# Two column groups of the recurrence moved from narrow blocks with stationary activations into one early wide block that TensorE turns

## The chip, the cores and the metric

The kernel runs on one core of a Trainium2 chip. The metric is the device time of one execution in microseconds (us); of the kernel before there are three runs, with a median of 1683.52. Engines are called as in the profile: PE (TensorE matmul), PEld (its weight load), DVE (VectorE), ACT (ScalarE), POOL (GpSimd) and SP (the queue that issues most DMAs).

## The reference

One decoder layer in float32 over 256 positions of width 2048. Cut to what matters:

```python
a = rmsnorm(h, norm_mix_pre)
proj = a @ w_in                       # 2048 x 17408
q_a, k_a, v_a, q_r, f_r, i_r, g_r, gate_a, gate_r = split_columns(proj)
attn = dilated_window_attention(...)  # three groups of 8 heads, rotary q and k
q_h = silu(q_r);  f = lb + (1 - lb) * sigmoid(f_r)
r_out = hgrn2_chunked(q_h, log(f), 1 - f, i_r)     # 8 heads of 128
r_out = rmsnorm(r_out) * gain * silu(g_r)
y = sigmoid(gate_a) * (attn @ w_attn_branch) + sigmoid(gate_r) * (r_out @ w_hgrn_branch)
h = h + rmsnorm(y @ w_mix_out)
g, u = split(rmsnorm(h) @ w_ffn_gate_up)
h = h + rmsnorm((silu(g) * u) @ w_ffn_down)
```

The row scale of the first norm is applied to the products, not to the operand. The change is about q_r and f_r, 1024 columns each, of which the kernel handles "half 0" (heads 0 to 3, 512 columns of each) and "half 1" apart.

## The kernel before, in words

All products are made in three matmuls of a high and a low part (x·w high, x·w low, low x·w high), so weights are split as they come in: ACT copies the high part out of the raw tile and DVE subtracts to get the low one (L355 and L356 for blocks of 256 columns, L390 and L410 for wide ones). The work is a list of blocks, each a list of steps over the contraction dimension; a step's matmuls are issued by `multiply` or `multiply_wide`, and behind each step the program advances the evacuations of finished blocks (`evacs`), two "lanes" of vector work (`lanes`, in which recurrence and attention run as generators, a piece a step), and, for steps in the range `ready_in`, one list of DMAs on POOL ("ready sums").

- A **wide block** (`Wide`) makes 1024 columns for all 256 positions in 8 steps. The activations are the stationary operand, so the result has positions on the partitions. A step "8" is 24 matmuls of 512 columns; a step "7" forms seven products of sums of quarters instead of eight (21 matmuls), which needs sums of weight quarters: SP loads the raw tile, POOL adds another quarter onto it with an accumulating DMA (L303), DVE adds (`sum`, L404 and L405), ACT and DVE split it into `dh` and `dl` (L415, L418). At the end of a block `gather` (L522 to L531) combines the seven products into a tile `e`, and `add_up` (L540) adds the others. Two sets of PSUM banks, `acc` and `aux`, change roles from block to block (`flip`). The early wide blocks make gate_a, gate_r, v and i; `evac_kept` (L812, L813) applies the function on ACT and writes `e` to DRAM by POOL ("kept"). From there it is read back (`back`, L803) when it is needed.
- A **W block** makes 256 columns in 4 steps of 512 rows with the weights stationary and the activations moving, so that the result has channels on the partitions and time along the row, as the recurrence and attention want it. A step is 16 matmuls. The blocks W#1 to W#4 are f and q_r of half 0 (`evac_f`, `evac_qr`), W#5 to W#8 those of half 1; 24 more make rotary q and k. At W#1 `end_early` closes the early stage's memory and opens the middle stage's, whose tiles take its place. At the end of W#4 `recurrence(0)` enters lane 0; its first DVE instruction makes kk = 1 − f (L1002).
- Then come the two branch products, the mix (`w_mix_out`, two wide blocks with POOL's raw additions) and the feed-forward stage (two narrow and ten wide blocks, then two wide ones of the down projection). In the feed-forward stage PE turns activations by transposes (L1454). Some of its seven steps use sums that were made in DRAM beforehand, the ready sums: three copies and three accumulating DMAs each, 256 KB a DMA (L446, L450), made in the 83 units from W#1 on that `ready_in` names. Their order against other POOL work is fixed by the place where the program issues them.

Of the kernel before, what the change touches and what calls it, by code (L numbers as in the profile page):

```python
# [39 lines left out]
def order(steps):  # L40

    k = steps.count("7")
    return [(steps[:i].count(x) + k * (x == "8"), int(x == "7")) for i, x in enumerate(steps)]


EARLY = [order(x) for x in ["88878878"] + ["87878787"] * 6 + ["88787878"]]
FFN = [order(x) for x in ["88878787"] + ["87877877", "87877877", "87877877", "87877877", "87877877", "87877877", "87877877", "87877877", "87877877"]]
DOWN = [[((n + 16 * j) % 22, n in by7) for n in range(KF // 2)] for j, by7 in enumerate( ([4, 6, 8, 10, 12, 14, 16, 18], [0, 2, 4, 6, 8, 10, 12, 14, 16, 18]))]

# [4 lines left out]


N_F = 16
KEPT_P, KEPT, KEPT_H = (18,), (6, 10), (16,)
READY, PACE, FIRST_READY, LAST_READY = {(2, 1), (2, 3), (3, 1), (3, 3), (4, 1), (4, 3), (5, 1), (5, 3), (6, 1), (6, 3), (7, 1), (7, 3), (8, 1), (8, 3), (9, 1), (9, 3), (10, 1), (10, 3), (11, 6), (11, 10), (11, 14), (12, 4), (12, 8), (12, 12), (12, 16)}, (4, 6), 2, 85


class Block:
# [48 lines left out]
def tile_hybrid_block(ctx: ExitStack, tc: tile.TileContext, t, out):  # L110
# [145 lines left out]
    def add_seven(*args, flip, whole=True, stage=None, **kw):  # L256
        b = Wide(*args, **kw)
        b.flip, b.whole, b.unit0, b.stage = flip, whole, len(units), stage
        b.plus = stage == "ffn"
        blocks.append(b)  # L260
        for i in range(b.steps):
            seq.append(Step(b, i, len(units), 0))
            units.append([seq[-1]])
# [309 lines left out]
    class Split:  # L573


        def __init__(self, s, nk, slot=rslot):
            self.flat = [slot(s) for _ in range(nk // 2)]
            self.slots = [x.rearrange("p (k z t) -> p k z t", k=2, z=2) for x in self.flat]
            self.there = set()

        def __call__(self, k):
            x = self.slots[k // 2]
# [222 lines left out]
    def evac_kept(key, fn):  # L805
        def go(b):
            dst = keep(key, 1024)
            add_up(b)
            yield
            for s in range(2):  # L810
                e = b.rest[:, 2 * s : 2 * s + 2].rearrange("p g c -> p (g c)")
                nc.scalar.activation(e, e, fn, scale=r1c[:, s : s + 1])  # L812
                nc.gpsimd.dma_start(dst[:, s, :], e)  # L813
                yield
        return go

    def end_early():
        flush(evacs)
        enter("middle")
        attnT.append(Split("attnT", 8))  # L820
        recT.append(Split("recT", 8))
        for half in range(2):
            gN[half] = hslot("g")
            back(gN[half], ("g", half), 0, 512, True)
            iN[half] = hslot("v")
            back(iN[half], "i", 512 * half, 512 * half + 512, True)
        for key, shape in (("lmask", [P, len(LEVELS), 64]), ("amask", [P, 2, 512])):
            masks[key] = pool["now"].tile(shape, F32, name=key)
            nc.gpsimd.dma_start(masks[key], t[key])

    def values_back(half):

# [11 lines left out]
    def evac_f(half):  # L844
        def ev(i, src):
            while "lb" not in ready:
                yield
            if i == 0:
                fT[half] = fslot("f").rearrange("p (h t) -> p h t", h=4)
            dst = fT[half]  # L850
            d = dst[:, 2 * i : 2 * i + 2, :]
            nc.vector.tensor_mul(in_time(d), by_side(src), by_side(by_rows(rowb, 2)))
            yield
            nc.scalar.activation(d, d, AF.Sigmoid)
            yield
            for h in (2 * i, 2 * i + 1):
                g = 4 * half + h
                nc.vector.tensor_scalar(
                    dst[:, h, :], dst[:, h, :], lb1[:, g : g + 1], lb[:, g : g + 1],
                    op0=OP.mult, op1=OP.add,  # L860
                )
        return ev

    def evac_qr(half, then=None):
        def ev(i, src):
# [119 lines left out]
    def recurrence(half):  # L985
# [175 lines left out]
        for j in range(2):  # L1161
            ps = aux()
            for h in range(2):
                for i in range(2):
                    hs = slice((2 * j + h) * P, (2 * j + h + 1) * P)
                    nc.tensor.transpose(
                        ps[:, h * S + i * P : h * S + (i + 1) * P], rt[:, i, hs], ident
                    )
            recT[0].put(2 * half + j, ps.rearrange("p (h t) -> p h t", h=2), True)
            if j == 1:  # L1170
                values_back(half)
            yield
# [258 lines left out]
    def aslot(s):  # L1431

        n = len(act_t)
        if len(H7) > 4 and n in (8, 9):
            x = hslot(s).rearrange("p b c -> p (b c)")
        else:
            x = rslot(s).bitcast(F32) if n < 8 else p3(s, F32, 1024, 1 if len(H7) > 4 else 3)
        return x.rearrange("p (k t) -> p k t", k=4)

    def turn_act(u, b):  # L1440

        dst = aslot("act")
        act_t.append(dst)
        side = "aux" if b.flip else "acc"
        pair = pair_of(side) if b.whole else [bank_of(side) for _ in range(2)]
        return lambda: turn_into(dst, pair, u, b.whole)
# [167 lines left out]
    for half in range(2):  # L1614
# [2 lines left out]
            post=more_x if half == 0 else None)  # L1617
    early = [(COL_GA, ("a", 0), AF.Sigmoid), (COL_GB, ("r", 0), AF.Sigmoid),
             (COL_GA + 1024, ("a", 1), AF.Sigmoid), (COL_GB + 1024, ("r", 1), AF.Sigmoid)]
    early += [(COL_V + 1024 * g, ("v", g), AF.Copy) for g in range(3)] + [(COL_IR, "i", AF.Copy)]  # L1620
    for n, (col, key, fn) in enumerate(early):
        add_seven(w_in, (col, col + 512), EARLY[n], xT, lambda m: x7[m],
                  evac_kept(key, fn), flip=n % 2 == 1, whole=n < 7, turn=1 if n else 6,
                  pre=({0: lambda: advance(evacs), 1: lambda: flush(lanes[1])}).get(n))
    for half in range(2):
        add_wide(w_in, KD, COL_FR + 512 * half, xT, evac_f(half))
        if half == 0:
            blocks[-2].pre = end_early
        add_wide(w_in, KD, COL_QR + 512 * half, xT, evac_qr(half, start_recurrence(half)))
    for pair in range(4):  # L1630
        for g in range(3):
            for o, col, tab in ((0, COL_Q, 0), (2, COL_K, 2)):
                then = start_attention(pair) if o and g == 2 else None
                add("W", w_in, KD, col + 1024 * g + 256 * pair, xT,
                    both_halves(evac_rope((pair, g), o, tab, then), 0))
    blocks[-3].pre = lambda: (gate_back("r", 0), gate_back("r", 1))
    for j in range(4):
        add("N", t["w_hgrn_branch"][0], 8, 512 * j, lambda k: recT[0](k), evac_rec_branch(j))
# [28 lines left out]
        st.n = n  # L1667
    for j, b in enumerate(blocks[mix_last + 3 :], 1):
        b.plus = any(k == j for k, _ in READY)
    ready_in = range(blocks[10].unit0 + FIRST_READY, blocks[10].unit0 + LAST_READY)  # L1670
    before = sums_before([
        st for st in seq if type(st.block) is Wide and (blocks.index(st.block) - mix_last - 2, st.i) in READY
    ])
    wide = [st.unit for st in seq if type(st.block) is Wide]
    extra.append(range(wide[0] + N_RAW, wide[0] + 64, N_RAW + 1))
    first = blocks[mix_last + 3].unit0 + N_RAW + 1
    extra.append(range(first, len(units) + N_RAW + 1, N_RAW + 1))

# [47 lines left out]
    for n, st in enumerate(seq):  # L1726
        b, i = st.block, st.i
        if n == mix_end:
            from_mix_to_ffn(n)
        if mix_end <= n < mix_end + 5:  # L1730
            continue
        if i in b.at:
            b.at[i]()
        if i == 0 and b.pre:
            b.pre()
        if n >= 2:
            rest = ahead(n)
            late = type(b) is Wide and i == b.last7 == b.steps - 1
            if not late:
                rest()  # L1740
        if n >= len(seq) - 3:
            continue
        if type(b) is Wide:
            if i == b.turn and b.order[i][1]:
                st.between = lambda: turn_act(turns.popleft(), b) if turns else None
            multiply_wide(st)
            flush(later)
            later.clear()
            if i == b.last7:
                gather(b)  # L1750
        else:
            multiply(st)
        if b.post:
            b.post(i)
        if n < 2:
            ahead(n)()
        advance(evacs)
        if turns and type(turns[0]) is not list:
            advance(turns)
        advance_lanes()  # L1760
        if st.unit in ready_in:
            next(before, None)
        if type(b) is not Wide:
            if st.last:
                evacs.append(b.evac(b.banks))
            continue
        if i == b.turn:
            flush(evacs)
            if turns:
                turn_act(turns.popleft(), b)()  # L1770
        if st.last:
            evacs.append(b.evac(b))
            advance(evacs)
            if late:
                rest()
# [63 lines left out]
```

## Time and profile before

| | us |
|---|---|
| median of 3 runs (lowest to highest) | 1683.52 (1683.25 to 1683.81) |
| profiled execution, device time | 1684.82 |
| its span | 1682.6 |
| PE busy, share of the span | 1670.8, 99% |
| DVE busy, share | 1425.6, 85% |
| ACT busy, share | 938.1, 56% |
| mean granted clock of PE | 0.998 |

"Busy" is the time in which an engine has an instruction in work; a busy PE is one with a matmul in flight, matmuls overlap, and so the distance between two starts tells more than the length of one. The granted clock is in shares of the full clock, 1.00 in all stretches quoted below. Starts are counted from the start of the span. Lines are those of the kernel before; in the changed kernel they are one higher at first, and more further down.

### The profile page before, as it was taken

Reading aid. Unit: us, or ns where it says so; the run is one execution under the profiler, and the core shown is the slowest. Engines: PE = TensorE matmul, PEld = TensorE weight load, DVE = VectorE, ACT = ScalarE, POOL = GpSimd, SP = SyncE. Lnnn points to the kernel's source line nnn. Section 1 sums busy time; section 2 is a strip of 40 time slices with the busy share of each in tenths; the row PEclk is TensorE's granted clock in tenths of the full one; section 3 lists DMA queues with packets and bytes.
Section 4 is the critical chain, followed back from the end, with each engine's and each line's share of the span. In section 5 each row is a group of like instructions: output and inputs, shape, how many; then the busy total and the mean of one; then the engine's idle time right before and its main releaser. Section 6 shows DMA issues by size and latency. Waiting matters only on the chain.

```text
span 1682.6 us, 21753 instructions
## 1 busy us (share of the span) xinstructions
PE 1670.8 (99%) x8178; PEld 1402.1 (83%) x8178; DVE 1425.6 (85%) x1497; ACT 938.1 (56%) x960; POOL 226.4 (13%) x311
## 2 busy tenths in 40 slices
PE   9999999999999999999999999999999999999997
PEld 7888888888888888888888888888888888888886
DVE  6888899985887987777668887999999999899988
ACT  6655555554535434544445565566666665666664
POOL 0111111102320331320200010111111111000100
PEclk9999999999999999999999999999999999999999
DMA  8788888778995997995947857998898888888893
GB/s 285 264 259 256 252 258 262 248 243 285 307 281 172 317 288 238 304 312 178 290 154 246 265 178 248 284 274 270 273 277 280 269 280 267 263 259 241 252 306 106
DMA packets 241881, 432.89 MB, mean 257 GB/s; under 512 B 15184, under 2 KB 81792, under 8 KB 241776
## 3 DMA queue, kind: packets, MB, share of 16 engines
q1 hardware_dynamic: 201808, 337.55, 59.6%
q0 software_dynamic: 37344, 88.03, 22.6%
q10 hardware_dynamic: 2624, 5.92, 1.1%
q8 instruction: 64, 1.05, 0.2%
q14 instruction: 41, 0.34, 0.1%
HBM read 418.34 MB, written 52.43 MB: 280 GB/s over the span
## 4 chain that ended last, share of the span: by engine, by line
PE 92%; DVE 4%; DMA 2%; issue 2%; ACT 1%; SPq 0%; DVEq 0%; ACTq 0%
PE acc L169 57%; PE aux L169 32%; DMA raw<-in_w_in 2%; DVE wl L410 2%; PE aux L966 0%; DVE dl L418 0%; PE aux L635 0%; PE acc L1454 0%; DVE fz L1586 0%; PE aux L1454 0%; ACT w L390 0%; DVE e L540 0%; PE aux L623 0%; ACT junk L1541 0%; DVE w L356 0%
## 5 line engine op out<-in xcount | busy, mean ns | idle before, releaser
L390 ACT ACTIVATE w<-raw 128x2048 fp32r<-128x2048 f32 x204 | 390.1, 1913 | 217.6 <-issue 71.0
L410 DVE TENSOR_TENSOR wl<-raw,w 128x2048 fp32r<-128x2048 f32 x204 | 465.0, 2286 | 22.8 <-ACT w L390 21.0
L169 PE MATMUL acc<-xT,w 128*128 128x256 f32 (+1 forms) x2048 | 369.8, 339 | 0.0
L169 PEld LDWEIGHTS acc<-xT,w 128*128 128x128 f32 x2048 | 312.0, 188 | 43.8
L356 DVE TENSOR_TENSOR w<-raw,w 128x1024 fp32r<-128x1024 f32 (+1 forms) x191 | 232.3, 1217 | 134.7 <-ACT w L355 133.7
L355 ACT ACTIVATE w<-raw 128x1024 fp32r<-128x1024 f32 (+1 forms) x191 | 200.9, 1053 | 227.4 <-PE acc L169 184.0
L415 ACT ACTIVATE dh<-sum 128x1536 fp32r<-128x1536 f32 x99 | 147.6, 1491 | 150.6 <-PE acc L169 55.3
L418 DVE TENSOR_TENSOR dl<-sum,dh 128x1536 fp32r<-128x1536 f32 x99 | 173.5, 1752 | 21.0 <-ACT dh L415 20.7
L169 PE MATMUL acc<-w,xT 128*128 128x512 f32 x522 | 154.2, 392 | 0.3 <-DVE w L356 0.2
L169 PE MATMUL acc<-w,hT 128*128 128x512 f32 x504 | 152.9, 391 | 0.0
L169 PE MATMUL aux<-w,hT 128*128 128x512 f32 x368 | 122.9, 389 | 0.0
L169 PEld LDWEIGHTS acc<-w,xT 128*128 128x128 f32 x522 | 97.1, 188 | 21.4 <-DVE w L356 1.2
L169 PE MATMUL aux<-w,xT 128*128 128x512 f32 x346 | 111.9, 389 | 0.0
L169 PEld LDWEIGHTS acc<-w,hT 128*128 128x128 f32 x504 | 94.0, 188 | 19.7 <-DVE w L356 0.4
L303 POOL DMA_DIRECT2D raw<-in_w_ffn_gate_up x48 | 42.3, 880 | 378.3 <-DMA raw<-in_w_ffn_gate_up 227.3
L169 PE MATMUL aux<-w,a 128*128 128x512 f32 x260 | 83.4, 389 | 0.0
L169 PEld LDWEIGHTS aux<-w,hT 128*128 128x128 f32 x368 | 69.1, 188 | 14.3
L169 PEld LDWEIGHTS aux<-w,xT 128*128 128x128 f32 x346 | 65.0, 188 | 13.4
L169 PE MATMUL acc<-w,a 128*128 128x512 f32 x228 | 73.3, 389 | 0.0
L169 PE MATMUL aux<-wl,hT 128*128 128x512 f32 x184 | 71.6, 389 | 0.0
L169 PE MATMUL acc<-w,so 128*128 128x512 f32 x182 | 70.9, 389 | 0.0
L169 PE MATMUL aux<-w,so 128*128 128x512 f32 x182 | 70.8, 389 | 0.0
(336 smaller groups left out, 2865.6 us busy)
## 6 DMA issues: line engine op xcount, KB each, us to landing
raw<-in_w_in SPq DMA_DIRECT2D x271, 512.0 KB, 6.1
raw<-in_w_ffn_gate_up SPq DMA_DIRECT2D x176, 512.0 KB, 5.1
raw<-in_w_ffn_down SPq DMA_DIRECT2D x88, 512.0 KB, 5.7
sum<-ready SPq DMA_DIRECT2D x25, 768.0 KB, 7.2
ready<-in_w_ffn_gate_up POOLq DMA_DIRECT2D x72, 256.0 KB, 6.9
raw<-in_w_mix_out SPq DMA_DIRECT2D x32, 512.0 KB, 5.4
ready<-ready POOLq DMA_DIRECT2D x50, 256.0 KB, 7.0
raw<-in_w_ffn_gate_up POOLq DMA_DIRECT2D x48, 256.0 KB, 6.1
```

The source lines that it names most:

```text
L169: nc.tensor.matmul(ps, lhsT, rhs, start=start, stop=stop, skip_group_check=True)
L303: nc.gpsimd.dma_start(raw[:, :512], rows, accum_op=OP.add)
L355: nc.scalar.activation(wh[:, k], raw[:, k], AF.Copy)
L356: nc.vector.tensor_sub(wl[:, k], raw[:, k], wh[:, k].bitcast(F32))
L390: nc.scalar.activation(hi, raw, AF.Copy)
L410: nc.vector.tensor_sub(lo, raw, hi.bitcast(F32))
L415: nc.scalar.activation(hi, flat, AF.Copy)
L418: nc.vector.tensor_sub(lo, flat, hi.bitcast(F32))
```

## The change

f and q_r of half 0 are no longer made by W#1 to W#4. One more early wide block, the eighth of nine, computes 512 columns of f_r beside 512 of q_r. Its evacuation `evac_fq` applies the row scale and the sigmoid in `e`, and leaves two entries in `turns`. In step 1 of the ninth early block (the third part of v, here "v2") `turn_fq` transposes `e` with 16 PE transposes of 128x128 into four PSUM banks, and ACT writes them out as f and q_r of half 0, channels on partitions, in slots of another pool (`rslot("fq")`). The change of stage memory (`end_early`) and the start of `ready_in` move to the first W block that is left, the former W#5; `recurrence(0)` enters lane 0 there and waits two steps. The ready range is 15 units longer at its end. The slots of `recT` are taken one at a time when they are needed. Half 1 stays as it was.

```diff
-EARLY = [order(x) for x in ["88878878"] + ["87878787"] * 6 + ["88787878"]]
+EARLY = [order(x) for x in ["88878878", "87878787", "87878787", "87878787", "87878787", "87878787", "87878787", "87878787", "88787878"]]
...
+WIDE_FQ, FLIP = 1, 1
...
-READY, PACE, FIRST_READY, LAST_READY = {(2, 1), (2, 3), (3, 1), (3, 3), (4, 1), (4, 3), (5, 1), (5, 3), (6, 1), (6, 3), (7, 1), (7, 3), (8, 1), (8, 3), (9, 1), (9, 3), (10, 1), (10, 3), (11, 6), (11, 10), (11, 14), (12, 4), (12, 8), (12, 12), (12, 16)}, (4, 6), 2, 85
+READY, PACE, FIRST_READY, LAST_READY = {(2, 1), (2, 3), (3, 1), (3, 3), (4, 1), (4, 3), (5, 1), (5, 3), (6, 1), (6, 3), (7, 1), (7, 3), (8, 1), (8, 3), (9, 1), (9, 3), (10, 1), (10, 3), (11, 6), (11, 10), (11, 14), (12, 4), (12, 8), (12, 12), (12, 16)}, (4, 6), 2, 100
...
     def end_early():
         flush(evacs)
         enter("middle")
         attnT.append(Split("attnT", 8))
-        recT.append(Split("recT", 8))
+        recT.append(Split("recT", 8, None))
...
+        for half in range(WIDE_FQ):
+            lanes[0].append(waiting(2, recurrence(half)) if half == 0 else recurrence(half))
...
+    def evac_fq(half):
+        def go(b):
+            add_up(b)
+            yield
+            e = b.rest
+            for s in range(2):
+                r, sig = r1c[:, s : s + 1], ptile("sig")
+                nc.scalar.activation(sig, e[:, 2 * s + 1], AF.Sigmoid, scale=r)
+                nc.scalar.activation(e[:, 2 * s], e[:, 2 * s], AF.Sigmoid, scale=r)
+                nc.vector.scalar_tensor_tensor(
+                    out=e[:, 2 * s + 1], in0=e[:, 2 * s + 1], scalar=r, in1=sig,
+                    op0=OP.mult, op1=OP.mult,
+                )
+                yield
+            for g in range(2):
+                turns.append([turn_fq(half, g, e)])
+        return go
+
+    def turn_fq(half, g, e):
+        def go(b):
+            side = "aux" if b.flip else "acc"
+            pair = pair_of(side) if b.whole else [bank_of(side) for _ in range(2)]
+            dst = (fT, qT)[g][half] = rslot("fq").bitcast(F32).rearrange("p (h t) -> p h t", h=4)
+            pss = [pair[:, i, :] if b.whole else pair[i] for i in range(2)]
+            for i, ps in enumerate(pss):
+                for kk in range(2):
+                    for s in range(2):
+                        at, c = kk * S + s * P, (2 * i + kk) * P
+                        nc.tensor.transpose(ps[:, at : at + P], e[:, 2 * s + g, c : c + P], ident)
+            for i, ps in enumerate(pss):
+                ps = ps.rearrange("p (k t) -> p k t", k=2)
+                if g:
+                    nc.scalar.activation(in_time(dst[:, 2 * i : 2 * i + 2, :]), by_side(ps), AF.Copy)
+                    continue
+                for kk in range(2):
+                    h = 4 * half + 2 * i + kk
+                    nc.scalar.activation(
+                        in_time(dst[:, 2 * i + kk : 2 * i + kk + 1, :]), by_side(ps[:, kk : kk + 1, :]),
+                        AF.Identity, scale=lb1[:, h : h + 1], bias=lb[:, h : h + 1],
+                    )
+        return go
...
-    early += [(COL_V + 1024 * g, ("v", g), AF.Copy) for g in range(3)] + [(COL_IR, "i", AF.Copy)]
-    for n, (col, key, fn) in enumerate(early):
-        add_seven(w_in, (col, col + 512), EARLY[n], xT, lambda m: x7[m],
-                  evac_kept(key, fn), flip=n % 2 == 1, whole=n < 7, turn=1 if n else 6,
+    early += [(COL_V, ("v", 0), AF.Copy), (COL_V + 1024, ("v", 1), AF.Copy), (COL_IR, "i", AF.Copy)]
+    early += list(range(WIDE_FQ)) + [(COL_V + 2048, ("v", 2), AF.Copy)]
+    for n, what in enumerate(early):
+        if type(what) is int:
+            cols, evac = (COL_FR + 512 * what, COL_QR + 512 * what), evac_fq(what)
+        else:
+            cols, evac = (what[0], what[0] + 512), evac_kept(*what[1:])
+        add_seven(w_in, cols, EARLY[n], xT, lambda m: x7[m],
+                  evac, flip=n % 2 == FLIP, whole=n < len(early) - 1, turn=1 if n else 6,
                   pre=({0: lambda: advance(evacs), 1: lambda: flush(lanes[1])}).get(n))
-    for half in range(2):
+    first_w = len(blocks)
+    for half in range(WIDE_FQ, 2):
         add_wide(w_in, KD, COL_FR + 512 * half, xT, evac_f(half))
-        if half == 0:
-            blocks[-2].pre = end_early
         add_wide(w_in, KD, COL_QR + 512 * half, xT, evac_qr(half, start_recurrence(half)))
...
+    blocks[first_w].pre = end_early
...
-    ready_in = range(blocks[10].unit0 + FIRST_READY, blocks[10].unit0 + LAST_READY)
+    ready_in = range(blocks[first_w].unit0 + FIRST_READY, blocks[first_w].unit0 + LAST_READY)
...
         if i == b.turn:
             flush(evacs)
-            if turns:
+            while turns:
                 turn_act(turns.popleft(), b)()
```

What the queues look like at three places. PE between steps 1 and 2 of the last early wide block, v2, in the changed kernel (`ident` is the identity, `e` the tile of f and q_r, `so` are sums of activations):

```order
L170 MATMUL aux_2947<-w_2868,xT_110 128x512 x2
L170 MATMUL aux_2947<-wl_2869,xT_110 128x512
L170 MATMUL aux_2947<-w_2868,xT_110 128x512
L904 MATMUL acc_2993<-ident,e_2892 128x128 x4
L904 MATMUL acc_2994<-ident,e_2892 128x128 x4
L904 MATMUL acc_3008<-ident,e_2892 128x128 x4
L904 MATMUL acc_3009<-ident,e_2892 128x128 x4
L170 MATMUL aux_2933<-w_2903,xT_106 128x512
L170 MATMUL aux_2933<-wl_2904,xT_106 128x512
```

The sixteen transposes stand between the products of an eight step and those of a seven step; no such rows are in the early stage before.

DVE around the first piece of the recurrence, before (W#5; `q` holds q_r, `f` the decay, `w` the low parts of the weights of W blocks):

```order
L356 TENSOR_TENSOR w_3342<-raw_3167,w_3342 128x1024 [waits DMAHW6_49,Activation_49]
L356 TENSOR_TENSOR w_3363<-raw_3214,w_3363 128x1024 [waits DMAHW7_49,Activation_49]
L874 TENSOR_TENSOR q_3239<-q_3239,sig_3335 128x512 [waits DVE_49]
L1002 TENSOR_SCALAR kk_3385<-f_3043 128x1024
L356 TENSOR_TENSOR w_3391<-raw_3214,w_3391 128x1024 [waits DMAHW0_49,Activation_49]
L1057 TENSOR_TENSOR x_3411<-kk_3385,q_3239 128x1024 [waits DMASW7_49,DMASW0_49,DVE_49]
```

and in the changed kernel, in the same block (`fq_2995` holds f, `fq_3010` q_r):

```order
L357 TENSOR_TENSOR w_3265<-raw_3064,w_3265 128x1024 [waits DMAHW6_49,Activation_49]
L357 TENSOR_TENSOR w_3285<-raw_3098,w_3285 128x1024 [waits DMAHW7_49,DVE_49,Activation_49]
L1056 TENSOR_SCALAR kk_3306<-fq_2995 128x1024 [waits DMASW4_49,DMASW3_49,DVE_49]
L357 TENSOR_TENSOR w_3311<-raw_3098,w_3311 128x1024 [waits DMAHW0_49,Activation_49]
L1111 TENSOR_TENSOR x_3331<-kk_3306,fq_3010 128x1024 [waits DVE_49]
```

The rows are nearly the same, but kk now waits for two of POOL's DMAs (the semaphores with SW in their names).

POOL in the mix, before (`raw` rows are additions onto raw weights of the mix, `ready` rows are ready sums, `h` is the residual sum behind the mix):

```order
L450 DMA ready_7088<-ready_7088 128x512
L450 DMA ready_7237<-ready_7237 128x512
L303 DMA raw_7462<-in_w_mix_out 128x512
L303 DMA raw_7519<-in_w_mix_out 128x512
L450 DMA ready_7237<-ready_7237 128x512
L303 DMA raw_7717<-in_w_mix_out 128x512
L303 DMA raw_7786<-in_w_mix_out 128x512
L1277 TENSOR_TENSOR h_8114<-zg_7829,hx_7747 128x256
```

and in the changed kernel:

```order
L304 DMA raw_7387<-in_w_mix_out 128x512
L451 DMA ready_7112<-ready_7112 128x512
L447 DMA ready_7409<-in_w_ffn_down 128x512 x3
L304 DMA raw_7449<-in_w_mix_out 128x512
L451 DMA ready_7258<-ready_7258 128x512
L451 DMA ready_7409<-in_w_ffn_down 128x512
L451 DMA ready_7258<-ready_7258 128x512
L447 DMA ready_7645<-in_w_ffn_down 128x512 x3
L304 DMA raw_7653<-in_w_mix_out 128x512
L451 DMA ready_7409<-ready_7409 128x512
L304 DMA raw_7723<-in_w_mix_out 128x512
L451 DMA ready_7645<-in_w_ffn_down 128x512
```

One ready sum DMA stood among the mix's raw additions; eleven do now, and three more follow behind the last one ahead of `h`.

More of the change, by code (lines that the diff above doesn't have):

```diff
@@ L576, in __init__, with grow @@
         def __init__(self, s, nk, slot=rslot):
-            self.flat = [slot(s) for _ in range(nk // 2)]
-            self.slots = [x.rearrange("p (k z t) -> p k z t", k=2, z=2) for x in self.flat]
-            self.there = set()
+            self.flat, self.slots, self.there = [], [], set()
+            for _ in range(nk // 2 if slot else 0):
+                self.grow(slot(s))
+        def grow(self, x):
+            self.flat.append(x)
+            self.slots.append(x.rearrange("p (k z t) -> p k z t", k=2, z=2))
         def __call__(self, k):
@@ L815, in evac_kept, with waiting @@
         return go
+    def waiting(n, lane):
+        for _ in range(n):
+            yield
+        yield from lane
     def end_early():
@@ L862, in evac_f @@
         return ev
+    def evac_fq(half):
[11 more added lines that the diff above has]
+                )
+                yield
+            for g in range(2):
[24 more added lines that the diff above has]
+        return go
     def evac_qr(half, then=None):
@@ L1168, in recurrence @@
                     )
+            recT[0].grow(rslot("recT"))
             recT[0].put(2 * half + j, ps.rearrange("p (h t) -> p h t", h=2), True)
@@ L1440, in turn_act @@
     def turn_act(u, b):
+        if len(u) == 1:
+            return lambda: u[0](b)
         dst = aslot("act")
@@ L1674, in tile_hybrid_block @@
     wide = [st.unit for st in seq if type(st.block) is Wide]
-    extra.append(range(wide[0] + N_RAW, wide[0] + 64, N_RAW + 1))
+    extra.append(range(wide[0] + N_RAW, wide[0] + 8 * len(early), N_RAW + 1))
     first = blocks[mix_last + 3].unit0 + N_RAW + 1
```

## The prediction

> **What bounds the kernel now.** I read the page first, then stretches of the span, then the waits of PE in them. The page:
>
> ```profile
> span 1682.6 us, 21753 instructions
> PE 1670.8 (99%) x8178; PEld 1402.1 (83%) x8178; DVE 1425.6 (85%) x1497; ACT 938.1 (56%) x960; POOL 226.4 (13%) x311
> PE 92%; DVE 4%; DMA 2%; issue 2%; ACT 1%; SPq 0%; DVEq 0%; ACTq 0%
> ```
>
> PE is busy for 1670.8 of 1682.6 us, and the chain that ended last is 92% PE. Whether that holds where the change works is told by the busy time in three stretches: one early wide block, the four W blocks of f and q_r of half 0 (W#1 to W#4) that follow the last early wide block, and the four of half 1 (W#5 to W#8). The last three rows are the mix, used further down. Columns: window, its length, then busy us (and instructions) of PE, PEld, DVE, ACT and POOL, the granted clock, DMA share, GB/s.
>
> ```profile
> 304.04:344.84 40.80, 40.80 (x182) 33.80 (x181) 35.08 (x24) 24.08 (x16) 3.79 (x5) 1.00 0.83 257
> 386.16:430.76 44.60, 44.60 (x258) 38.92 (x257) 26.18 (x31) 21.23 (x26) 14.74 (x23) 1.00 1.00 320
> 430.76:475.35 44.59, 44.59 (x260) 39.01 (x259) 40.02 (x54) 22.66 (x30) 16.46 (x24) 1.00 1.08 315
> 905.00:925.00 20.00, 20.00 (x94) 16.56 (x93) 16.26 (x13) 10.73 (x8) 1.75 (x2) 1.00 0.89 265
> 925.00:945.00 20.00, 20.00 (x89) 16.55 (x89) 15.04 (x13) 7.01 (x5) 0.90 (x1) 1.00 0.97 323
> 945.00:965.00 20.00, 20.00 (x90) 16.56 (x89) 17.92 (x14) 13.13 (x15) 0.90 (x1) 1.00 0.72 213
> ```
>
> PE is busy all of each stretch, at the full granted clock. The waits of PE from 40 to 1045 us come to 1.5 us in all:
>
> ```profile
> PE aux L169 <- DVE wl L410: 0.9, 2, 0.6
> PE acc L169 <- DVE wl L410: 0.6, 1, 0.6
> ```
>
> So up to the feed-forward stage time is what PE has to issue. A change that takes matmuls away there is paid in full, as long as nothing new makes PE wait.
>
> **The change part by part. Removed:** four W blocks. PE issues each K-step of a W block as 16 matmuls, 8 of 512 and 8 of 256 columns; 4 steps make 64, four blocks 256. Their pitch:
>
> ```profile
> 386.16 67.04 PE L169 MATMUL acc<-xT,w 128*128 128x512 f32 x384
> 453.04 0.40 PE L169 MATMUL aux<-hi,ones 128*128 128x512 f32 x1
> ```
>
> 384 matmuls from 386.16 to 453.04 are 66.88 us, 0.1742 us each; 256 of them are 44.59 us. That is 11.15 us a block.
>
> **Added:** one early wide block in the pattern 8-7-8-7-8-7-8-7: four steps of 24 matmuls and four seven-product steps of 21, all of 512 columns, 180 in all. Two blocks of that pattern start in the chain of waits at
>
> ```profile
> 232.64 6.80 PE aux L169 x30
> 273.44 6.80 PE acc L169 x30
> ```
>
> so one takes 273.44 − 232.64 = 40.80 us (0.2267 us a matmul), the length of the first stretch above as well. The bare exchange is 40.80 − 44.59 = −3.79 us.
>
> **Added:** 16 transposes of 128x128 on PE, in step 1 of the next wide block (v2). The kernel has such transposes in the feed-forward stage, 8 at a time:
>
> ```profile
> L1454 PE MATMUL aux<-ident,e x40: 270/272/273, 1082.9 to 1412.5; 128*128 128x128 f32 x40
> 1082.90 1.03 PE L1454 MATMUL aux<-ident,e 128*128 128x128 f32 x8
> 1083.69 0.48 PE L169 MATMUL aux<-dh,so 128*128 128x512 f32 x1
> 1084.01 0.40 PE L169 MATMUL aux<-dl,so 128*128 128x512 f32 x1
> 1083.06 0.87 PE aux L1454 x8
> ```
>
> One lasts 272 ns, but 8 take 0.79 us from their first start to the next matmul's start (1083.69 − 1082.90), which itself runs 0.09 us behind the usual 0.23 pitch; the chain gives 0.87 us for 8. Sixteen cost 1.6 to 1.74 us if pipelined, 16 × 0.272 = 4.35 us if not. I take 1.7, the row of the same operation and size. Sum: −3.79 + 1.7 = **−2.1 us**.
>
> The Trainium skill, "TensorE: Matmul & The Clock Gate", section "Part 4: PE-mode transpose", speaks against this change: about 275 ns for a transpose inside a kernel, and the full clock does not engage for that mode. By it, were they serial, the sum would be −3.79 + 16 × 0.275 = +0.6 us, an estimate. The trace agrees on the length of one (272 ns) but has eight in 0.79 to 0.87 us, and grants the full clock in a stretch that holds eight of them:
>
> ```profile
> 1075.58:1116.68 41.10, 41.10 (x186) 33.98 (x186) 37.82 (x29) 25.32 (x17) 4.40 (x5) 1.00 0.91 274
> ```
>
> **Moved, at the boundary fq to v2.** The evacuation of the new block adds, on DVE ahead of v2's second seven, two products of 128x512, and four ACT sigmoids. The like boundary of before:
>
> ```profile
> 345.45 2.35 DVE L540 TENSOR_TENSOR e<-aux,e 128x1024 f32<-128x1024 f32 x2
> 347.72 2.28 DVE L410 TENSOR_TENSOR wl<-raw,w 128x2048 fp32r<-128x2048 f32 x1
> 438.80 0.68 DVE L874 TENSOR_TENSOR q<-q,sig 128x512 f32<-128x512 f32 x1
> ```
>
> Two such products, by the nearest row (0.68 us), cost 1.3 us of DVE; in the stretch 304.04 to 344.84 DVE is busy 35.08 of 40.80, so 5.7 us are free to cover them. They stand behind the low part wl that PE needs first. If the cover were gone, they cost 1.3 us; before, these waits were 0.6 us at most in a row. Six ACT evictions of the transposes go into an ACT that is busy 24.08 of 40.80 us. I add 0.2 us for it all (0 to 1.3).
>
> **Moved, at the first W block that is left** (W#5 of before). The middle stage's memory opens there, not at W#1, and the recurrence of half 0 starts two W steps in. Its first DVE instruction, kk, now writes where v2's kept tiles were read out by two POOL DMAs, and so waits for them; behind it in DVE's queue stand the splits of W's weights, which PE waits for.
>
> ```profile
> 388.64 0.53 POOL L813 DMA_DIRECT2D kept<-e  x1 [2.21 <-ACT e L812]
> 439.40 0.69 DVE L1002 TENSOR_SCALAR kk<-f 128x1024 f32<-128x1024 f32 x1
> kept<-e POOLq DMA_DIRECT2D x2, 512.0 KB, 3.2
> DMA to landing us min/median/max: 2.9/7.9/10.1
> 463.53 0.70 DVE L1122 TENSOR_TENSOR kk<-kk,tot 128x512 f32<-128x512 f32 x1
> 465.58 1.89 PE L169 MATMUL aux<-q,kk 128*128 128x64 f32 x16
> ```
>
> Before, the second kept tile of the last wide block went out 2.5 us after W#1's start (388.64 − 386.16) and landed in 3.2 us: 5.7 after it. kk ran 8.64 us after the start of W#5 (439.40 − 430.76), and about the same number of steps into W#5 is where it now stands. With a landing of 3.2 us it does not wait at all. Over the kernel these landings had a median of 7.9 and a largest of 10.1 us: kk would be held 10.4 − 8.6 = 1.8 or 12.6 − 8.6 = 4.0 us, and the nearest need of PE for its successor has 465.58 − (463.53 + 0.70) = 1.35 us to spare. That is 0 to 2.7 us of PE; I take 0, since the last two kept tiles are the same place.
>
> **Moved, the ready sums on POOL.** They start at the first W block that is left, which starts 40.8 + 1.7 = 42.5 us after 386.16, where they started before; so that 14 of POOL's ready DMAs (256 KB each) now stand between the first raw addition of the mix and h, where one did. Each raw addition of POOL there waits for an SP transfer, and DVE waits for it. The rows of POOL, DVE and PE, then the issues of two windows (905 to 955, then 431 to 475):
>
> ```profile
> 912.50 1.18 POOL L450 DMA_DIRECT2D ready<-ready  x1
> 940.59 0.90 POOL L303 DMA_DIRECT2D raw<-in_w_mix_out  x1 [26.92 <-DMA raw<-in_w_mix_out]
> 947.31 0.69 DVE L404 TENSOR_TENSOR sum<-raw 128x512 f32<-128x512 f32 x1 [1.52 <-DMA raw<-in_w_mix_out]
> 952.61 1.76 DVE L418 TENSOR_TENSOR dl<-sum,dh 128x1536 fp32r<-128x1536 f32 x1 [0.32 <-ACT dh L415]
> 956.35 0.39 PE L169 MATMUL acc<-dl,so 128*128 128x512 f32 x1
> raw<-in_w_mix_out SPq DMA_DIRECT2D x18, 512.0 KB, 7.1
> raw<-in_w_in SPq DMA_DIRECT2D x15, 512.0 KB, 8.3
> ```
>
> POOL's queue has room (27 us of waiting at 940.59). What can be late is data: the second mix block's first seven step has dl ready at 954.37 and uses it at 956.35, 1.98 us to spare. Two transfers in a row stand ahead of it (SP's, then POOL's addition, 940.59 to 947.31 = 6.7 us). If each lands as in the W stage, where ready sums run (8.3 instead of 7.1), they are 2 × 1.2 = 2.4 us late and PE loses 0.4. Both ends: 0, and the rival below. I take 0.1.
>
> **Sum:** −2.1 + 0.2 + 0.1 = −1.8 us, rounded so: span 1680.8. The profiled execution, 1684.82 us, is 2.2 above its span and 1.3 above the median of the runs shown (1683.52); taken from that median, **1681.7 us**.
>
> **The rivals.**
>
> *A, the forecast:* PE stays filled, −1.8; 1680.3 to 1683.0 by the bounds of the boundary (0 to 1.3), the transposes (1.6 to 1.74) and a partial stall in the mix. For it: no PE wait above 0.6 us before 1045.
>
> *B, the mix is starved, slower.* Place: the first seven step of each mix block; price: what its two transfers in a row exceed 1.98 us of slack. For it: 905 to 945 already moves 0.89 to 0.97 of the DMA engines' time, and 13 more ready DMAs of 256 KB are 3.4 MB, at 323 GB/s 10.5 us of all engines. Against it: 945 to 965 is at 0.72, and PE's weights are queued ahead. If each transfer takes the largest landing above, 10.1 for 6.7, each chain is 6.8 us late, less 1.98 is 4.8; at one block: 1683.52 − 1.8 + 4.8 = 1686.5; at both, up to +9.6, 1691.3. It decides the sign once the stalls pass 1.8 us, and is slower by the 0.2% from 5.2 on.
>
> *C, kk held by the kept tiles:* +0.5 to +2.7, 1682.2 to 1684.4. For it: the median landing over the kernel; against: the 3.2 of the very place.
>
> *D, serial transposes:* −3.79 + 4.35 + 0.3 = +0.9, 1684.4. Against it: eight start within 0.8 us in the feed-forward stage. For it: here they stand four to a bank and not eight to a pair.
>
> *E, more than counted:* four blocks of a DMA share of 1.00 to 1.08 become one of 0.83, and DVE's early recurrence has less ahead of it; but PE waits only 1.5 us in all that can be regained before 1045, giving 1680.2, so it would take waits of later stages as well: 1679.
>
> **How the numbers follow.** A 0.66, B 0.17 (0.10 of it slower by over 0.2%), C 0.05, D 0.03, E 0.09. 0.2% is 3.37 us, about what a measurement of this kernel can tell from no change: 1680.15 and 1686.89 are the bounds. Faster by over it takes 1.5 us more than the sum: E, 0.09; slower: B's upper part and a little of all else, 0.11; within: 0.80. The forecast is 1681.7; its own range 1680.3 to 1683.0. Until 0.2 is left out, the range takes in C, D and B's partial stall: 1680.0 to 1685.5.
>
> **What would show it.** The early part: nine wide blocks of which the new one is 40.8 us long, with the start of the first W block 40.8 + 1.7 us later than 386.16 (about 428.7), and kk as far behind it as it was behind W#5 before. Wrong if transposes take over 2 us from the first to the next matmul; if PE has a wait on wl in v2's steps 1 and 2; on w at L357 within 10 us of the first W block (C); on dl or wl in the mix between 915 and 965 (B). A branch stage that ends about 2 us earlier than before, with a total no earlier, makes the mix or the feed-forward stage the place; one that does not end earlier makes the sum wrong.

## The result and the profile after

| | before | changed |
|---|---|---|
| median, 16 runs each (us) | 1684.55 | 1687.89 |
| lowest to highest | 1683.25 to 1686.09 | 1686.76 to 1695.39 |
| profiled execution, its span | 1684.82, 1682.6 | 1687.21, 1685.4 |

The ratio is 1.0023, with a 95% interval of 1.0016 to 1.0031: the change made the kernel slower by 0.23%, some 3.3 us in the medians and 2.8 us between the two profiled spans. The forecast was 1.8 us faster; 1687.89 lies above its range.

The page of the changed kernel, head, engines and chain:

```profile
span 1685.4 us, 21641 instructions
PE 1671.6 (99%) x8118; PEld 1400.0 (83%) x8118; DVE 1436.8 (85%) x1490; ACT 944.1 (56%) x955; POOL 230.8 (14%) x315
PE 84%; DVE 7%; DMA 4%; issue 3%; ACT 1%; SPq 0%; DVEq 0%; ACTq 0%; POOLq 0%
```

There are 60 matmuls fewer, as there should be (256 less, 180 and 16 more), yet PE is busy 0.8 us longer, and the chain of waits holds DVE and DMA for 11% instead of 6%. Where the time went is seen by following the same instructions through both traces. The first and last starts of some groups, in the changed kernel (the W blocks; the products with the difference sums `dh` in the mix's first and second block; the feed-forward stage's products of `hT`, the activations there, that go to `acc`):

```profile
L170 PE MATMUL acc<-xT,w x1792: 274/337/497, 428.6 to 797.8; 128*128 128x512 f32 x100, 128*128 128x256 f32 x100
L170 PE MATMUL acc<-dh,yT x4: 389/389/389, 919.3 to 930.0; 128*128 128x512 f32 x4
L170 PE MATMUL aux<-dh,yT x4: 389/389/389, 960.2 to 970.8; 128*128 128x512 f32 x4
L170 PE MATMUL acc<-w,hT x504: 387/389/490, 988.7 to 1447.0; 128*128 128x512 f32 x168
```

and in the kernel before:

```profile
L169 PE MATMUL acc<-dh,yT x4: 389/389/389, 921.4 to 932.1; 128*128 128x512 f32 x4
L169 PE MATMUL aux<-dh,yT x4: 389/389/389, 958.2 to 968.8; 128*128 128x512 f32 x4
L169 PE MATMUL acc<-w,hT x504: 387/389/504, 985.8 to 1444.2; 128*128 128x512 f32 x168
```

The changed kernel is 2.1 us ahead when W#5 starts (428.6 against 430.76), and still 2.1 ahead at the last of these products in the first mix block (930.0 against 932.1). At the first seven step of the second mix block it is 2.0 behind (960.2 against 958.2), at the first of the feed-forward products 2.9 behind (988.7 against 985.8), and that stays: 2.8 at the last of that group (1447.0 against 1444.2) and at the end of the span. So the whole loss, 4.1 + 0.9 = 5.0 us, arises between 930 and 989, in the mix. PE there, in the changed kernel:

```profile
952.07 0.70 PE L170 MATMUL aux<-w,yT 128*128 128x512 f32 x2
954.60 0.50 PE L170 MATMUL aux<-wl,yT 128*128 128x512 f32 x1 [1.83 <-DVE wl L411]
956.88 0.63 PE L170 MATMUL acc<-wl,yT 128*128 128x512 f32 x1
957.31 0.63 PE L170 MATMUL acc<-w,yT 128*128 128x512 f32 x1
959.04 0.39 PE L170 MATMUL acc<-dl,so 128*128 128x512 f32 x1
986.76 0.59 PE L1348 MATMUL acc<-ident,h 128*128 128x128 f32 x2 [0.59 <-DVE h L1334]
```

PE waits 1.83 us for wl. What comes behind is unlike anything in the profile before: matmuls start 0.43 us apart (956.88 to 957.31) instead of 0.23. Twelve intervals from 954.60 to 959.04 take 4.44 us instead of 12 × 0.2267 = 2.72. The granted clock of four windows (columns as in the prediction's table of stretches) shows it:

```profile
954.00:955.00 1.00, 0.40 (x2) 0.36 (x3) 1.00 (x2) 1.00 (x2) 1.00 (x3) 1.00 0.00 0
956.00:957.00 1.00, 1.00 (x4) 0.79 (x3) 1.00 (x1) 1.00 (x1) 0.42 (x1) 0.50 1.17 129
957.00:958.00 1.00, 1.00 (x4) 0.81 (x3) 0.95 (x2) 0.83 (x3) 0.00 (x0) 0.50 0.91 217
959.00:960.00 1.00, 1.00 (x6) 0.80 (x6) 1.00 (x2) 1.00 (x1) 0.00 (x0) 1.00 1.10 358
```

The clock was halved for 3.41 us, from 955.14 to 958.56. So the 4.1 us are the wait (2.30 between two starts instead of 0.23: 2.1 us), the slow matmuls (1.7 us) and small hitches (0.2 us at 941, 0.1 us at 952). The page counts the slow matmuls as busy time, which is why PE's waits grew less than the span.

Why wl was late is on POOL and DVE:

```profile
901.83 2.29 POOL L447 DMA_DIRECT2D ready<-in_w_ffn_down  x3
923.69 1.90 POOL L447 DMA_DIRECT2D ready<-in_w_ffn_down  x3
942.00 0.93 POOL L304 DMA_DIRECT2D raw<-in_w_mix_out  x1 [16.41 <-DVE wl L411]
950.17 0.69 DVE L405 TENSOR_TENSOR sum<-raw 128x512 f32<-128x512 f32 x1 [2.40 <-DMA raw<-in_w_mix_out]
952.25 2.29 DVE L411 TENSOR_TENSOR wl<-raw,w 128x2048 fp32r<-128x2048 f32 x1
raw<-in_w_mix_out SPq DMA_DIRECT2D x16, 512.0 KB, 9.5
```

The last row is the issue table between 905 and 955: the mix's raw tiles take 9.5 us to land, where they took 7.1. POOL's addition is issued at 942.00; 2.1 us ahead of before it would have been 938.5. It lands in 8.2 us (950.17 − 942.00) instead of 6.7. DVE has its data 5.0 us later than it should (950.17 against 947.31 − 2.13), and wl had 2.6 us to spare (951.68 against its first use at 954.30 in the kernel before). The last tiles of the mix are late in the same way, so h, which follows them on DVE, makes PE wait at 986.76: the 0.9 us.

### The profile page after: what moved, and what is told of

The parts are those of the page before. It is cut to its first block, busy times and chain, and to the rows that moved or that the text cites. A ratio compares the mean times of both kernels' runs of the same rounds, so it can differ in the third digit from the quotient of the medians.

```text
span 1685.4 us, 21641 instructions
## 1 busy us (share of the span) xinstructions
PE 1671.6 (99%) x8118; PEld 1400.0 (83%) x8118; DVE 1436.8 (85%) x1490; ACT 944.1 (56%) x955; POOL 230.8 (14%) x315
## 4 chain that ended last, share of the span: by engine, by line
PE 84%; DVE 7%; DMA 4%; issue 3%; ACT 1%; SPq 0%; DVEq 0%; ACTq 0%; POOLq 0%
PE acc L170 52%; PE aux L170 30%; DVE wl L411 3%; DMA raw<-in_w_in 3%; DMA raw<-in_w_mix_out 1%; DVE dl L419 1%; ACT w L391 1%; DVE e L541 0%; PE aux L1020 0%; PE aux L640 0%; PE acc L1511 0%; DVE fz L1643 0%; DVE sum L406 0%; DVE e L532 0%; DVE sum L405 0%
## 5 line engine op out<-in xcount | busy, mean ns | idle before, releaser
L391 ACT ACTIVATE w<-raw 128x2048 fp32r<-128x2048 f32 x212 | 405.7, 1914 | 236.8 <-issue 80.8
L411 DVE TENSOR_TENSOR wl<-raw,w 128x2048 fp32r<-128x2048 f32 x212 | 483.5, 2287 | 25.4 <-ACT w L391 23.0
L170 PE MATMUL acc<-xT,w 128*128 128x512 f32 (+1 forms) x1792 | 325.2, 339 | 0.0
L357 DVE TENSOR_TENSOR w<-raw,w 128x1024 fp32r<-128x1024 f32 (+1 forms) x175 | 212.8, 1217 | 116.8 <-ACT w L356 115.8
L170 PEld LDWEIGHTS acc<-xT,w 128*128 128x128 f32 x1792 | 273.1, 188 | 38.1
L356 ACT ACTIVATE w<-raw 128x1024 fp32r<-128x1024 f32 (+1 forms) x175 | 184.1, 1053 | 202.9 <-PE acc L170 166.0
L419 DVE TENSOR_TENSOR dl<-sum,dh 128x1536 fp32r<-128x1536 f32 x103 | 180.6, 1753 | 22.3 <-ACT dh L416 22.0
L170 PE MATMUL aux<-w,xT 128*128 128x512 f32 x434 | 140.0, 389 | 0.0
L170 PEld LDWEIGHTS aux<-w,xT 128*128 128x128 f32 x434 | 81.5, 188 | 16.8
L170 PE MATMUL aux<-wl,xT 128*128 128x512 f32 x217 | 84.7, 390 | 0.8 <-DVE wl L411 0.6
```

Source lines behind the costliest of these rows:

```text
L170: nc.tensor.matmul(ps, lhsT, rhs, start=start, stop=stop, skip_group_check=True)
L356: nc.scalar.activation(wh[:, k], raw[:, k], AF.Copy)
L357: nc.vector.tensor_sub(wl[:, k], raw[:, k], wh[:, k].bitcast(F32))
L391: nc.scalar.activation(hi, raw, AF.Copy)
L411: nc.vector.tensor_sub(lo, raw, hi.bitcast(F32))
L419: nc.vector.tensor_sub(lo, flat, hi.bitcast(F32))
```

## The experiments

The theory after the result: the ready sums that the change moved into the mix put bytes on the DMA engines there, the mix's raw tiles land late, PE waits, and the wait takes the clock down. Rivals: the mix is late for another reason that came with the change; POOL's order and not the bytes; the saving of 2.1 us is not real and something else hides it.

**The ready sums earlier.** One number of the changed kernel:

```diff
-READY, PACE, FIRST_READY, LAST_READY = {...}, (4, 6), 2, 100
+READY, PACE, FIRST_READY, LAST_READY = {...}, (4, 6), -14, 100
```

> The changed kernel with one number different: the ready sums start 16 units earlier, in the last but one early wide block, so that about as many of them stand ahead of the mix as before the change (one among the mix's raw additions instead of eleven). Theory (the ready sums that moved into the mix make its raw transfers late, and that costs the 5 us): the landings of the mix's raw tiles fall from 9.5 us towards 7.1, PE does not wait for wl at 954, and the time is that of before less about 2 us (ratio 0.9985 to 0.9995). Rival 1 (the mix is late for another reason, such as memory that moved or the order on SP): still 2 to 4 us over before. Rival 2 (ready sums only move the harm, now into the early wide blocks with their own raw additions on POOL): no wait in the mix, but waits for wl between 340 and 430, and no gain.

Measured: 1682.42 us (11 runs) against 1684.72 (27 runs), ratio 0.9985 (0.9976 to 0.9994). The window 953 to 961, the waits of PE over the whole span and the mix's landings between 905 and 955:

```profile
953.00:961.00 8.00, 8.00 (x37) 6.64 (x36) 7.92 (x7) 5.51 (x6) 0.00 (x0) 1.00 0.68 231
PE aux L170 <- DVE wl L411: 0.7, 1, 0.7
PE acc L170 <- DVE wl L411: 0.5, 1, 0.5
raw<-in_w_mix_out SPq DMA_DIRECT2D x16, 512.0 KB, 7.1
```

The tiles land in 7.1 us again, PE and its clock are full, and the span is 1680.4, 2.2 us below the span before; the prediction's count for PE was 2.1. So Rival 1 falls. Of the two waits for wl that are left, one of 0.7 us at 56 has its like in the prediction's table of waits. The other, 0.5 us at 350, is what Rival 2 named: between 340 and 430 neither the kernel before nor the changed kernel has a wait. It is small, the gain is there all the same, and Rival 2 falls with it.

**The ready sums denser.**

```diff
-READY, PACE, FIRST_READY, LAST_READY = {...}, (4, 6), 2, 100
+READY, PACE, FIRST_READY, LAST_READY = {...}, (3, 5), 2, 100
```

> The changed kernel with the ready sums started where the change starts them, but made denser: an addition every 3 steps instead of 4, a new one every 5 instead of 6, so that all are issued ahead of the mix's first raw addition. Theory: as for the earlier start, before less about 2 us. Rival 2, in the W stage: DMA is at a share of 1.0 there already, the weights of W blocks land later, PE waits for DVE's w rows and the gain is lost; 1 us or more of PE waits between 430 and 800.

Measured: 1682.15 us, ratio 0.9985 (0.9976 to 0.9994), span 1680.2. In the W stage between 500 and 780 the raw tiles land in 8.3 us where they took 7.0, as the rival had it, but PE has no wait there: W blocks had that much to spare.

**Its partner: the denser pace on the kernel before.**

```diff
-READY, PACE, FIRST_READY, LAST_READY = {...}, (4, 6), 2, 85
+READY, PACE, FIRST_READY, LAST_READY = {...}, (3, 5), 2, 85
```

> The kernel before with the denser ready sums (3 and 5 steps for 4 and 6) and nothing else: the partner of the changed kernel with that pace. If the change itself is worth the 2.1 us that PE saves, this stays within 1 us of before and the changed kernel with that pace is 2 us below it. If the denser pace brings the gain (one ready DMA less in the mix), this is about 2 us below before too.

Measured: 1684.38 us against 1684.91, ratio 0.9998 (0.9989 to 1.0007). The pace alone does nothing that can be told; the gain of the run above is the change's.

**The ready sums late, and nothing else, on the kernel before.**

```diff
-READY, PACE, FIRST_READY, LAST_READY = {...}, (4, 6), 2, 85
+READY, PACE, FIRST_READY, LAST_READY = {...}, (4, 6), 10, 108
```

> The kernel before with one thing of the change alone: its ready sums start at W#5 instead of W#1 (8 units later) with the longer range, which puts POOL's queue in the mix into the order of the changed kernel. Theory: 4 to 6 us slower than before (ratio 1.0025 to 1.0035), with a wait for wl near 955 and a granted clock below 1 behind it. Rival 1 (the cause is in the rest of the change): within 1 us of before.

Measured: 1689.97 us, ratio 1.0035 (1.0022 to 1.0048), 5.3 us above before; the span is 1688.2. The waits of PE:

```profile
PE aux L169 <- DVE wl L410: 3.0, 4, 1.6
PE acc L1293 <- DVE h L1279: 1.3, 1, 1.3
PE acc L169 <- DVE dl L418: 0.3, 1, 0.3
```

The mix's raw tiles land in 9.5 us here too. So this one piece of the change, without a wide block or a transpose, costs as much as the changed kernel lost. The clock expectation failed in this profile: behind a wait of 1.59 us the matmuls were 0.23 apart. The loss is made of waits alone; the one on h is longer than in the changed kernel (1.3 us for 0.6).

**The bytes or the order.** The changed kernel, POOL's queue unchanged, with fewer columns in the last five ready sums:

```diff
+            few = 16 if len(steps) < 5 else 512
...
-            mid, row, all4 = (st.ready[:, n * 512 : (n + 1) * 512] for n in range(3))
+            mid, row, all4 = (home[:, n * 512 : n * 512 + few] for n in range(3))
```

> The changed kernel, its POOL queue instruction for instruction as it is, but the last five ready sums (those whose DMAs fall into and just ahead of the mix) move 16 columns instead of 512, and the steps that would use them read an earlier sum of the same size instead: so five weight sums of the down projection are wrong, and all else is unchanged. It tells bytes from order. If the loss comes from the bytes that these DMAs put on the DMA engines: the mix's raw tiles land in about 7 us again, no wait for wl near 954, 1.5 to 2.5 us below before. If it comes from POOL's order (a raw addition stands behind ready DMAs that wait): still 3 us over before.

Measured: 1682.06 us against 1684.91, ratio 0.9982 (0.9973 to 0.9991). The issues between 905 and 955 and the window:

```profile
raw<-in_w_mix_out SPq DMA_DIRECT2D x18, 512.0 KB, 6.4
ready<-ready POOLq DMA_DIRECT2D x5, 8.0 KB, 6.1
953.00:961.00 8.00, 8.00 (x37) 6.63 (x36) 7.96 (x7) 4.73 (x3) 0.64 (x1) 1.00 0.70 224
```

As many DMAs in the same places, with 8 KB in each instead of 256, and the loss is gone: it is the bytes.

**What a wait of PE costs.** The four probes are the kernel before with more DVE work ahead of wl in the first seven step of the second mix block; its transfers are untouched:

```diff
-        nc.vector.tensor_sub(lo, raw, hi.bitcast(F32))
+        for _ in range(3 if b is blocks[mix_last] and st.i == 2 else 1):
+            nc.vector.tensor_sub(lo, raw, hi.bitcast(F32))
```

> The kernel before, its transfers untouched, with DVE's low part wl made three times over in the first seven step of the second mix block: 2 x 2.29 = 4.58 us more of DVE ahead of wl (3.3 us to spare) and dl (2.0 to spare). It asks what a short wait of PE costs. Theory (a wait of 2 us takes the granted clock down for some 4 us behind it, which costs about 2 us more): PE idle 2.6 us, matmuls behind it 0.43 apart for 4 us, the time 4 to 5 us over before. Rival (the wait costs what it lasts, and the slow matmuls in the changed kernel come from something else, such as the DMA load): 2.6 us over before, no slow matmuls.

Measured: 1688.91 us (10 runs, 1685.34 to 1690.78), ratio 1.0021 (1.0012 to 1.003). By the trace of before wl had 2.6 us to spare and not 3.3. The profiled execution is the shortest of the ten, 1685.34: there the data came early, PE waited 0.95 us, and the clock stayed. The other nine, 1.7 to 6.1 us over the median of before, have no profile, and these losses lie on both sides of what the theory and the rival said, so this run alone doesn't tell the one from the other.

Four times instead of three:

> As the first DVE probe on the kernel before, but wl made four times in that step: 3 x 2.29 = 6.87 us more of DVE. PE idle by about 3 to 3.3 us where the first probe's profile had 0.95 and 0.2. If a wait of about 2 us takes the granted clock down behind it: matmuls 0.43 us apart for some 4 us after the wait, the granted clock near 0.8 in an 8 us window, 2 us lost on top of the wait. If not: 0.23 apart right behind it.

Measured: 1692.17 us (3 runs), ratio 1.0044 (1.0029 to 1.0059). PE, then two windows:

```profile
958.71 0.80 PE L169 MATMUL aux<-wl,yT 128*128 128x512 f32 x1 [3.81 <-DVE wl L411]
960.16 0.63 PE L169 MATMUL aux<-wl,so 128*128 128x512 f32 x1
960.58 0.63 PE L169 MATMUL aux<-w,so 128*128 128x512 f32 x1
957.00:958.00 1.00, 0.00 (x0) 0.00 (x0) 1.00 (x1) 0.00 (x0) 0.00 (x0) 1.00 0.00 0
960.00:961.00 1.00, 1.00 (x3) 0.72 (x3) 1.00 (x2) 0.00 (x0) 0.00 (x0) 0.50 0.78 231
```

The transfers were those of before, the share of DMA was 0.00 while PE waited, and the clock was halved all the same: it follows the wait, not the DMA load. The slow matmuls end at 961.44 and cost 1.4 us here, less than the 2 that were expected. Two lengths between, as single runs:

> The first DVE probe (wl three times in the first seven step of the second mix block, kernel before) with one more subtraction of 512 columns, 0.69 us: PE's wait for wl near 1.6 us, between the 1.59 us that left the clock alone in the kernel before with late ready sums and the 1.83 us behind which the changed kernel ran at half the pitch. If length alone decides, matmuls behind it are 0.23 apart up to about 1.7 us of waiting and 0.43 apart beyond; if not, the two cases come out mixed.

> The same with two more such subtractions, 1.38 us: a wait near 2.3 us. If length alone decides: matmuls 0.43 apart behind it for 2 to 4 us, granted clock about 0.8 in the window of 8 us, and 1 to 2 us lost on top of the wait.

Measured: 1688.12 and 1686.73 us, beside one run of before of 1685.93 on that chip. The first probe's wait and the matmul behind it:

```profile
956.56 0.50 PE L169 MATMUL aux<-wl,yT 128*128 128x512 f32 x1 [1.81 <-DVE wl L411]
956.90 0.40 PE L169 MATMUL aux<-w,yT 128*128 128x512 f32 x1
957.14 0.40 PE L169 MATMUL aux<-w,so 128*128 128x512 f32 x1
```

The second missed its length: its wait fell apart into 0.75 and 1.36 us, with the clock at 1.00. The changed kernel again:

> The changed kernel once more, for a second profile. Theory: the same place loses again (a wait for wl of 1 to 3 us at the first seven step of the second mix block, raw tiles of the mix landing in 9 us or more), in all 4 to 6 us between 930 and 990; whether the slow clock comes with it depends on the length of the wait.

Measured: 1689.38 us, span 1687.6; the mix's raw tiles land in 9.4 us, and the same place loses:

```profile
956.54 0.78 PE L170 MATMUL aux<-wl,yT 128*128 128x512 f32 x1 [1.82 <-DVE wl L411]
957.11 0.63 PE L170 MATMUL aux<-w,yT 128*128 128x512 f32 x1
957.54 0.63 PE L170 MATMUL aux<-w,so 128*128 128x512 f32 x1
```

1.81 us of waiting left the clock alone in one run and 1.82 us halved it in another. So the length alone does not decide at this size.

**Where the wait lies.** The traces show what decides beside the length. The granted clock changes only at the ends of periods of 3.413 us. In the changed kernel it fell at 955.14, rose at 958.56 and fell again at 1678.77, when the work was done: one period, then 211. In its second profile it was 956.59, 960.00 and 1683.63, in the long probe 958.17, 961.58 and 1685.21: one period, then 212, both times. In all twelve traces the time from the first rise of the clock to its first fall is a whole number of periods, 278 to 491. Where the periods lie in the span differs from execution to execution: the first rise stands 4.0 to 6.9 us behind the start. Counted from these points, the periods around the waits are (columns as above; the second number after the window is PE's busy time):

```profile
951.73:955.14 3.41, 1.58 (x7) 0.93 (x6) 3.28 (x3) 3.41 (x8) 1.33 (x3) 1.00 0.37 143
955.15:958.55 3.40, 3.40 (x9) 2.67 (x8) 3.05 (x2) 2.68 (x4) 1.27 (x2) 0.50 0.87 178
953.17:956.58 3.41, 1.58 (x7) 0.77 (x5) 3.29 (x3) 3.41 (x8) 0.85 (x2) 1.00 0.54 205
956.59:960.00 3.41, 3.41 (x8) 2.73 (x9) 3.05 (x3) 3.19 (x4) 1.76 (x3) 0.50 0.70 128
952.86:956.27 3.41, 1.89 (x9) 1.23 (x7) 3.38 (x2) 3.41 (x4) 0.00 (x0) 1.00 0.05 9
956.27:959.69 3.42, 2.50 (x10) 1.75 (x11) 3.39 (x5) 0.69 (x1) 0.00 (x0) 1.00 0.31 84
954.79:958.20 3.41, 1.82 (x8) 1.24 (x7) 3.09 (x3) 3.41 (x8) 2.34 (x3) 1.00 0.32 78
```

The first two rows are the changed kernel, the next two its second profile: the whole wait lies in one period, PE is idle for 1.83 us of it, and the next period runs at half the clock. The fifth and sixth row are the probe that waited 1.81 us: a period ended at 956.27, within the wait, so that 1.5 us of idle time fell into one period and 0.9 us (with a later wait for dl) into the next, and the clock stayed. The last row is the kernel before with late ready sums, 1.59 us idle in one period, and the clock stayed. In the twelve traces, from the first rise to the fall at the end of the work, the clock fell behind every period with 1.83 us or more of idle PE and behind none with 1.59 us or less. No trace has a period between the two.

## Why the prediction was wrong

**The exchange of blocks: right.** W#5 starts at 428.63 in the changed kernel; the prediction said about 428.7. The 16 transposes:

```profile
396.27 1.91 PE L904 MATMUL acc<-ident,e 128*128 128x128 f32 x16
397.93 0.48 PE L170 MATMUL aux<-w,xT 128*128 128x512 f32 x1
```

take 1.66 us plus the 0.09 of a late start, for which the sum had 1.7. The rival of serial transposes did not occur, nor what was drawn for it from the Trainium skill, "TensorE: Matmul & The Clock Gate", section "Part 4: PE-mode transpose": the granted clock was 1.00 during the sixteen.

**The boundary fq to v2: right in sign, a little too dear.** PE has no wait between 340 and 440; the two products (1.41 us on DVE) were covered, for which 0.2 us had been added.

**kk behind the kept tiles: right.** The two kept tiles landed in 3.2 us, and kk ran at 436.69, 8.06 us after W#5's start, without being held.

**The ready sums in the mix: the step that failed.** The term "I take 0.1" of that step measured 5.0 us. Its mechanism, place and direction were those of rival B, at one block, whose price was set at 4.8 us of stall (1686.5); it was given 0.17. That 4.8 lies so near 5.0 is chance: it stood for one stall, and that stall was 2.1 us; the rest came from the clock, from h and from the hitches. Three sizes in the step were wrong:

- The landings were taken from the W stage, 8.3 us, as if the mix with ready sums were like it. They were 9.5 us, and the share of the DMA engines there rose to 1.0 without a break (945 to 953: 1.01 where before had 0.74). The mix has POOL's raw additions and the loads of x and of the norm's gain in the same stretch; whether these make the difference from the W stage is not shown.
- Two transfers in a row were each taken 1.2 us late. In fact the first chain link was 3.5 us late (942.00 against 938.5, held until the split of another tile gave its slot back), the second 1.5 us: lateness was carried from tile to tile through the slots, which the step, looking at one tile, left out.
- A wait was priced at its own length. In the changed kernel it cost 2.1 us and another 1.7 at the halved clock. The prediction had no term for that, though every window that it read stood at 1.00 only because PE never waited. And the tail of the mix, h, was not looked at: 0.9 us.

The observation that spoke against B, DMA at a share of 0.72 between 945 and 965, was read as room. The 3.4 MB filled it, but the tiles that were late had been issued ahead of it, between 905 and 945, where the share was 0.89 to 0.97 and there was hardly any.

**Rival E:** no gain beyond the sum was found; with the ready sums out of the mix the spans are 2.2 and 2.4 us below before, for 1.8 forecast and 2.1 from PE's count.

**What stays open:** where in the periods of the clock the waits of the executions without a profile fell, and so how the 3.3 us of the medians divide between waits and slow matmuls from run to run; and at how much idle time between 1.59 and 1.83 us of a period the clock falls.

## What to carry to other kernels

A change that shortens a stage by a fraction of a per cent should be followed to everything whose place is counted from that stage: here a queue of background copies started 42 us later, and its tail fell into the one stage whose transfers had 2 us to spare. Where the share of DMA is already as high as here (0.89 to 0.97), price added bytes by how late the whole row of tiles becomes, not by one tile's landing. Give a wait of PE of about 2 us a second price for the slow matmuls that may follow, here up to 1.7 us; whether it is paid depends on where the wait falls, so it differs between executions. The change was good for 2.3 us in the medians (ratio 0.9985) once the copies had been moved out of the mix by one number.

## What the runs showed of the hardware

Inside an otherwise unbroken stream the granted clock fell to 0.50 for one period of 3.41 us at waits of 1.82, 1.83 and 3.81 us, and PE ran at half rate in it, matmuls of 512 columns 0.43 us apart instead of 0.23; at waits of 0.95, 1.36, 1.59 and 1.81 us it did not. The clock changed at the ends of periods of 3.413 us alone, and fell where PE had been idle for 1.83 us or more of one. With a DMA share of 0.00 during the wait (the long probe) it fell the same way.

The Trainium skill, "TensorE: Matmul & The Clock Gate", section "What's actually happening", has the half clock as the state after at least one idle window of about 3.4 us. The two states, the halved rate and the length of the window agree with the traces. That a whole window has to be idle does not: 1.83 us of idle time in one was enough in the two profiles of the changed kernel, while 1.59 us, and a wait of 1.81 us that lay across the end of one, were not.
